# First stage of a two-layer denoising step: modulation by scale columns on TensorE, shift columns on VectorE, and another order of loads

## The chip, the cores and the metric

One core of a Trainium2 chip runs the whole kernel. The metric is device time in microseconds (us), the median of a few executions; lower is better. The core has five engines that each work through their own list in program order: TensorE (PE in the rows; PEld is its weight load), VectorE (DVE), ScalarE (ACT), GpSimd (POOL) and SyncE (SP), which issues the loads.

## The reference

Two groups of tokens (128 context tokens and 256 latent tokens, 384 together) pass through two layers. The part that the change touches is the first of three sub-layers of layer 0:

```
mod  = silu(cond) @ w_mod[l] + b_mod[l]          # cond: one vector of 1024 for each of the 2 groups
h    = x * (1 + mod[scale]) + mod[shift]         # scale and shift: 1024 values each
x    = LN(alpha*x + 0.5*mod[gate] * swiglu(h, w_ffn_in, w_ffn_out))
```

All of it is float32. The kernel makes the large products out of three products of a rounded type: weights and activations are split into a high part and a remainder (`wh` and `wl`, `xh` and `xl`), and `wh*xh + wl*xh + wh*xl` is summed.

## The kernel before

Activations lie with the 1024 features on 8 tiles of 128 partitions (k = 0 to 7) and the 384 tokens along the row. Weights arrive as units of 128 x 1024 in tiles named `raw`, a ring of 8. For a unit u, ScalarE casts `raw` to `wh` (L345) and VectorE subtracts to get `wl` (L353); TensorE then runs 24 products of 128x384, three for each k (L407, L408, L409). `take(n)` prepares units up to n. `dma_w(n)` issues unit loads up to n. All loads of this stage are issued by SyncE in program order; a load that reuses a ring slot waits for the last reader of that slot, and the loads behind it wait too.

The first stage, `first_group`, has to make scale and shift before it can multiply. It goes in four blocks b = 0 to 3 of 256 features (two tiles k each). For a block, `mod_mm` multiplies the conditioning vector `scz` with four loaded pieces of `w_mod` (L980, float32, 8 products of 512 columns for scale and shift together); ScalarE copies the result out of PSUM (`mr`, L987), `mod_sel` turns rows into columns on TensorE (L991), VectorE adds the bias (`ab`, L994 and L995), and `split_mod` makes `xh` on ScalarE (L843) and `hf` and then `xl = hf - xh` on VectorE (L850, L854). `main(u0, u1, k0, k1)` runs the products of units u0 to u1-1 for tiles k0 to k1-1. Seven units belong to the stage: 7 x 24 = 168 products. The order is written out by hand at the end of `first_group`, the products of ready tiles standing between the steps of the modulation.

Later modulation columns come from VectorE: a `w_mod` tile is multiplied with `scb`, the silu of the conditioning vector spread over all partitions, and summed along the row (`mod_dve`, two instructions of L454, one for each group, with a short read of the accumulator). `scb` is loaded by two broadcast loads in `start_rest` and passed through silu on ScalarE (L957).

Of the kernel before, what the change touches and what calls it, by code (L numbers as in the profile page):

```python
# [173 lines left out]
def _pack_mod(a, jobs):  # L174
    out = np.zeros((len(jobs), 128, 1024), np.float32)
    for n, (s, j, mode) in enumerate(jobs):
        l, i = divmod(s, 3)
        c0 = 3 * i * D + 128 * j
        w = a["w_mod"][l]
        if mode == "dve":  # L180
            out[n] = w[:, c0:c0 + 128].T
        else:
            b = j - 4096
            out[n] = np.stack([_blk(w, 2 * mode, 2, i0 + 256 * b, 256).reshape(128, 2, 256) for i0 in (0, D)],
                              axis=2).reshape(128, 1024)
    return out
# [35 lines left out]
C_ID, C_COS, C_SIN, C_INV, C_SEL = 0, 128, 384, 640, 640 + 784  # L222
# [17 lines left out]
class Kernel:  # L240
# [684 lines left out]
    def start(self):  # L925
        nc, io = self.nc, self.io
        self.P = self.t([128, NPAR], name="P")
        self.C = self.t([128, NCONST], name="C")
        self.X = self.t([128, 8, NT], name="X")
        self.scb = self.t([128, 2, 1024], name="scb")  # L930
        self.junk = self.t([128, 1024], BF16, name="junk")
        self.scz = self.t([128, 8, 32], name="scz")
        self.scT = self.scz[:, :, 0:2]
        self.sel = self.C[:, C_SEL:C_SEL + 2]
        self.ones = self.t([128, 1], name="ones")
        self.ident = self.C[:, C_ID:C_ID + 128]
        nc.vector.memset(self.scz, 0.0)
        nc.vector.memset(self.ones, 1.0)
        nc.sync.dma_start(self.P[:, 0:16], io["params"][:, 0:16])
        self.first = [[self.mod_dma(0, 4096, q) for q in range(3)]]  # L940
        nc.sync.dma_start(self.C[:, C_SEL:NCONST], io["const"][:, C_SEL:NCONST])
        nc.sync.dma_start(self.P[:, 16:PC["lng", 0, 0]], io["params"][:, 16:PC["lng", 0, 0]])
        self.first[0].append(self.mod_dma(0, 4096, 3))
        nc.sync.dma_start(self.X[:, 0:2, :], io["x"][:, 0:2, :])
        nc.scalar.activation(self.scT, self.P[:, 0:16].rearrange("p (k c) -> p k c", c=2), AF.Silu)

    def start_rest(self):

        nc, io = self.nc, self.io
        for c in range(2):  # L950
            nc.sync.dma_start(self.scb[:, c, :], io["cond"][c:c + 1, :].to_broadcast([128, D]))
            self.dma_w(self.n_dma + 1)
        nc.sync.dma_start(self.P[:, PC["lng", 0, 0]:NPAR], io["params"][:, PC["lng", 0, 0]:NPAR])
        nc.sync.dma_start(self.C[:, 0:C_SEL], io["const"][:, 0:C_SEL])

        def silu(c):
            nc.scalar.activation(self.scb[:, c, :], self.scb[:, c, :], AF.Silu)  # L957
        self.at(1, lambda: silu(0))
        self.at(1, lambda: silu(1))

    def first_group(self, l, j):

        nc = self.nc
        ab = self.pool.tile([128, 2, 8, 2], F32, name=self.nm("ab"), tag="ab", bufs=2)
        bm = self.par(("bmod", 0), 32).rearrange("p (j c) -> p j c", c=2)
        keys = [("ffn_in", l, j, c) for c in (0, NF, 1, NF + 1, 2, NF + 2, 3)]
        outs = [self.bank() for _ in range(6)] + [self.sbank("mm")]
        mm = nc.tensor.matmul
        ws, xs, psb = [], [], {}

        def load(b):
            self.first.append([self.mod_dma(0, 4096 + b, q) for q in range(4)])
            nc.sync.dma_start(self.X[:, 2 * b:2 * b + 2, :], self.io["x"][:, 2 * b:2 * b + 2, :])

        def mod_mm(b, half):
            if half == 0:
                psb[b] = self.sbank("m0")
            for k in range(4 * half, 4 * half + 4):
                g = 32 * (k % 4)
                mm(psb[b][g:g + 32, :], self.scz[:, k, :],  # L980
                   self.first[b][k // 2][:, 512 * (k % 2):512 * (k % 2) + 512], start=k < 4, stop=k >= 4)

        def mod_sel(b):
            ps = psb[b]
            row = [self.slot(name="mr") for _ in range(2)]
            for h in range(2):
                nc.scalar.copy(row[h][:, 0:256], ps[:, 256 * h:256 * h + 256])  # L987
            sv = self.sbank("m1")
            for h in range(2):
                for c in range(2):  # L990
                    mm(sv[:, 4 * h + 2 * c:4 * h + 2 * c + 2], row[h][:, 128 * c:128 * c + 128], self.sel,  # L991
                       start=True, stop=True)
            s2 = slice(2 * b, 2 * b + 2)
            nc.vector.tensor_add(ab[:, 1, s2, :], sv[:, 0:4].rearrange("p (k c) -> p k c", c=2), bm[:, 2 * b:2 * b + 2])  # L994
            nc.vector.scalar_tensor_tensor(ab[:, 0, s2, :], sv[:, 4:8].rearrange("p (k c) -> p k c", c=2), 1.0,  # L995
                                           bm[:, 8 + 2 * b:10 + 2 * b], ALU.add, ALU.add)
            fin = [self.split_mod(self.X[:, k, :], ab, k) for k in (2 * b, 2 * b + 1)]
            xs.extend(f() for f in fin)

        def main(u0, u1, k0, k1):  # L1000
            for u in range(u0, u1):
                (wh, wl), o = ws[u], outs[u]
                for k in range(k0, k1):
                    sl = slice(128 * k, 128 * k + 128)
                    self.mm3(o[:, :NT], wh[:, sl], wl[:, sl], xs[k][0], xs[k][1], k == 0, k == 7)

        def take(n):
            ws.extend(self.group(keys[len(ws):n]))
            self.held = min(n, self.NW)

        self.dma_w(2)
        load(1)
        self.dma_w(5)
        mod_mm(0, 0)
        mod_mm(0, 1)
        mod_sel(0)
        take(2)
        load(2)
        self.dma_w(7)
        main(0, 1, 0, 2)  # L1020
        mod_mm(1, 0)
        mod_mm(1, 1)
        main(1, 2, 0, 1)
        mod_sel(1)
        main(1, 2, 1, 2)
# [12 lines left out]
        self.dma_w(8)
        self.start_rest()
        main(0, 2, 4, 6)  # L1040
        mod_mm(3, 0)
        mod_mm(3, 1)
        main(2, 4, 4, 6)
        mod_sel(3)
        main(4, 7, 4, 6)
# [668 lines left out]
```

## Time and profile before

| | us |
|---|---|
| median of 3 runs | 1728.32 (1727.93 to 1728.36) |
| the profiled execution | 1728.01 |
| its span | 1726.2 |
| what lies around the span | 1.8 |
| TensorE busy | 1692.5 (98%) |
| the 168 products of the first stage | from 15.8 to 59.1 |

The profiled execution agrees with the runs within 0.3 us, so durations of the trace may be added to the median. TensorE is the engine of the chain that ended last for 90% of the span. A busy share near 100% does not say that TensorE does needed work all the time: the products of the modulation count as busy too.

### The profile page before, as it was taken

What the parts mean: (1) busy time and instruction counts of PE and PEld (TensorE: products, weight loads), DVE (VectorE), ACT (ScalarE), POOL (GpSimd) and SP (SyncE); (2) the same over time, 40 slices, a digit from 0 to 9 for tenths busy, and PEclk for the clock granted to TensorE, in tenths of its full rate; (3) what the DMA queues carried; (4) which work ended last, traced back from release to release, by engine and by line L of the source; (5) the groups of instructions that cost most, each with busy time, mean ns of one, the idle gap of its engine ahead of it and who ended that gap; (6) DMA issues with size and microseconds to landing.
All of it is one profiled execution on the core that took longest, in us unless ns stands there. A gap on an engine that the chain in (4) does not pass through costs nothing.

```text
span 1726.2 us, 26047 instructions
## 1 busy us (share of the span) xinstructions
PE 1692.5 (98%) x9734; PEld 1665.3 (96%) x9734; DVE 1321.2 (77%) x2241; ACT 769.5 (45%) x1369; POOL 342.9 (20%) x410
## 2 busy tenths in 40 slices
PE   7999999999998999999999999999999999999997
PEld 4999999999998999999999999999999999999997
DVE  3699998799959688889777888968998677653433
ACT  3523333656553473333374333347466337433322
POOL 0000023243214510002320000425221363000022
PEclk9999999999999999999999999999999999999998
DMA  9677776435534247676636766753444333544320
GB/s 375 241 236 231 235 233 210 131 110 162 146 114 135 62 140 238 209 213 207 200 99 211 214 206 208 221 160 107 145 138 131 111 116 92 171 148 124 119 75 37
DMA packets 86638, 287.44 MB, mean 167 GB/s; under 512 B 10096, under 2 KB 17520, under 8 KB 86512
## 3 DMA queue, kind: packets, MB, share of 16 engines
q1 hardware_dynamic: 86512, 285.79, 53.2%
q8 instruction: 76, 1.25, 0.3%
q14 instruction: 50, 0.41, 0.1%
HBM read 280.51 MB, written 2.62 MB: 164 GB/s over the span
## 4 chain that ended last, share of the span: by engine, by line
PE 90%; DVE 6%; ACT 2%; issue 1%; DMA 0%; SPq 0%; POOL 0%; ACTq 0%; DVEq 0%; POOLq 0%
PE mm L407 26%; PE mm L408 26%; PE mm L409 26%; DVE wl L353 3%; PE mm L731 1%; PE mm L732 1%; PE mm L734 1%; PE mm L429 1%; PE mm L432 1%; PE mm L430 1%; DVE acc L1117 1%; ACT wh L345 1%; PE m L980 1%; PE sm L539 1%; PE tot L546 1%
## 5 line engine op out<-in xcount | busy, mean ns | idle before, releaser
L345 ACT CAST wh<-raw 128x1024 fp32r<-128x1024 f32 (+3 forms) x430 | 400.3, 948 | 689.8 <-issue 444.2
L407 PE MATMUL mm<-xh,wh 128*128 128x384 f32 x1796 | 608.7, 339 | 4.1 <-ACT wh L345 3.1
L408 PE MATMUL mm<-xh,wl 128*128 128x384 f32 x1796 | 607.1, 338 | 0.6 <-DVE wl L353 0.6
L409 PE MATMUL mm<-xl,wh 128*128 128x384 f32 x1796 | 606.3, 338 | 0.1
L353 DVE TENSOR_TENSOR wl<-raw,wh 128x1024 fp32r<-128x1024 f32 (+3 forms) x430 | 489.8, 1154 | 112.4 <-ACT wh L345 112.2
L407 PEld LDWEIGHTS mm<-xh,wh 128*128 128x128 f32 x1796 | 337.8, 188 | 8.3 <-ACT wh L345 4.1
L408 PEld LDWEIGHTS mm<-xh,wl 128*128 128x128 f32 x1796 | 337.9, 188 | 1.9 <-DVE wl L353 1.8
L409 PEld LDWEIGHTS mm<-xl,wh 128*128 128x128 f32 x1796 | 337.6, 188 | 0.7 <-DVE xl L854 0.7
L454 DVE SCALAR_TENSOR_TENSOR junk<-raw,scb 128x1024 bf16<-128x1024 f32 x256 | 312.7, 1222 | 4.5
L409 PE MATMUL mm<-al,wh 128*128 128x384 f32 x704 | 237.5, 337 | 0.0
L407 PE MATMUL mm<-ah,wh 128*128 128x384 f32 x704 | 237.5, 337 | 0.0
L408 PE MATMUL mm<-ah,wl 128*128 128x384 f32 x704 | 237.3, 337 | 0.0
L625 POOL TENSOR_SCALAR sq<-sq 128x384 f32<-128x384 f32 x6 | 8.5, 1423 | 775.0 <-ACT sq L622 767.3
L409 PEld LDWEIGHTS mm<-al,wh 128*128 128x128 f32 x704 | 132.3, 188 | 0.0
L408 PEld LDWEIGHTS mm<-ah,wl 128*128 128x128 f32 x704 | 132.3, 188 | 0.0
L407 PEld LDWEIGHTS mm<-ah,wh 128*128 128x128 f32 x704 | 132.2, 188 | 0.0
L875 DVE TENSOR_TENSOR al<-a,ah 128x384 fp32r<-128x384 f32 x88 | 48.6, 557 | 80.2 <-ACT ah L874 76.6
L870 DVE TENSOR_TENSOR a<-mm,si 128x384 f32<-128x384 f32 x82 | 45.5, 556 | 75.9 <-ACT si L868 71.0
L1117 DVE SCALAR_TENSOR_TENSOR acc<-U,P,acc 128x399 f32<-128x399 f32 x120 | 87.5, 781 | 0.0
L631 POOL TENSOR_TENSOR s<-s,X 128x384 f32<-128x384 f32 x30 | 39.6, 1320 | 148.9 <-DVE X L611 126.2
L854 POOL TENSOR_TENSOR xl<-hf,xh 128x384 fp32r<-128x384 f32 x40 | 44.6, 1130 | 102.9 <-DVE t L792 84.8
L661 DVE SCALAR_TENSOR_TENSOR yl<-X,ab,yh 128x128 fp32r<-128x128 f32 x80 | 58.7, 770 | 6.2 <-ACT yh L659 6.0
(284 smaller groups left out, 2067.9 us busy)
## 6 DMA issues: line engine op xcount, KB each, us to landing
raw<-in_units SPq DMA_DIRECT2D x356, 512.0 KB, 3.9
raw<-in_wmod SPq DMA_DIRECT2D x144, 512.0 KB, 4.5
raw<-in_units SPq DMA_DIRECT2D x32, 384.0 KB, 3.8
X<-in_x SPq DMA_DIRECT2D x4, 384.0 KB, 7.0
K<-K SPq DMA_DIRECT2D x16, 96.0 KB, 4.3
out_y<-X SPq DMA_DIRECT2D x8, 192.0 KB, 1.8
scb<-in_cond SPq DMA_DIRECT2D x2, 512.0 KB, 7.3
Q<-QL SPq DMA_DIRECT2D x16, 64.0 KB, 3.9
```

The source lines that it names most:

```text
L345: self.nc.scalar.copy(w[0][:, c], r[:, c])
L353: self.nc.vector.tensor_sub(wl[:, c], r[:, c], wh[:, c].bitcast(F32))
L407: mm(out, wh, xh, start=first, stop=False)
L408: mm(out, wl, xh, start=False, stop=False)
L409: mm(out, wh, xl, start=False, stop=last)
L454: self.nc.vector.scalar_tensor_tensor(self.junk, r, 1.0, self.scb[:, c, :], ALU.mult, ALU.mult, accum_out=mv[:, j, c:c + 1])
L631: nc.gpsimd.tensor_add(st["s1"], st["s1"], x)
L661: nc.vector.scalar_tensor_tensor(lo[:, a:b], x[:, a:b], self.ab[:, 0, m, c:c + 1], h[:, a:b].bitcast(F32), ALU.mult, ALU.subtract)
L854: (nc.gpsimd if pool else nc.vector).tensor_sub(xl, hf, xh.bitcast(F32))
L870: nc.vector.tensor_mul(a, u[:, :NT], sl)
L875: nc.vector.tensor_sub(lo, a, h.bitcast(F32))
L1117: nc.vector.scalar_tensor_tensor(acc[c][:, :399], U[c][:, j:j + 399], w, acc[c][:, :399], ALU.mult, ALU.add)
```

## The change

Block 0 is as before (512 columns, scale and shift by TensorE), but for blocks 1 to 3 TensorE multiplies for the scale alone (`scale_mm`, 8 products of 256 columns, two loaded pieces in place of four), and the six shift tiles j = 2 to 7 are each a `w_mod` tile loaded in the transposed form (`col`) and summed by VectorE (`dot`, that is `mod_dve`). For that, `scb` is needed early: `spread` makes it by 16 products of 128 columns on TensorE, a column of `scz` repeated 128 times against the identity, and VectorE copies the result from PSUM. The two broadcast loads of 512 KB and the two silu passes go away; the identity (64 KB) is loaded early. `xl` is made by GpSimd in place of VectorE. `main` runs all `wh` products of a unit ahead of its `wl` products. The third unit's cast and subtraction are taken ahead of the second block.

```diff
-        self.first = [[self.mod_dma(0, 4096, q) for q in range(3)]]
+        self.first = [self.mod_dma(0, 4096, 0)]
+        nc.sync.dma_start(self.C[:, 0:128], io["const"][:, 0:128])
+        self.first += [self.mod_dma(0, 4096, q) for q in (1, 2, 3)]
...
-        for c in range(2):
-            nc.sync.dma_start(self.scb[:, c, :], io["cond"][c:c + 1, :].to_broadcast([128, D]))
...
+        def spread(c, half):
+            b = self.bank()
+            for n in range(4):
+                k = 4 * half + n
+                mm(b[:, 128 * n:128 * n + 128], self.scz[:, k, c:c + 1].to_broadcast([128, 128]), self.ident,
+                   start=True, stop=True)
+            nc.vector.tensor_copy(self.scb[:, c, 512 * half:512 * half + 512], b)
...
+        def scale_mm(b):
+            ps = self.sbank("m0")
+            for k in range(8):
+                g = 32 * (k % 4)
+                mm(ps[g:g + 32, 0:256], self.scz[:, k, :], chunks[b][k // 4][:, 256 * (k % 4):256 * (k % 4) + 256],
+                   start=k < 4, stop=k >= 4)
+            return ps
...
+        def split(k):
+            xs.append(self.split_mod(self.X[:, k, :], ab, k, False, True)())
...
+                for n, (i, w) in enumerate(((0, wh), (1, wh), (0, wl))):
+                    for k in range(k0, k1):
+                        mm(o[:, :NT], w[:, 128 * k:128 * k + 128], xs[k][i], start=n == 0 and k == 0,
+                           stop=n == 2 and k == 7)
...
+        take(3)
+        self.dma_w(4)
+        dot(3)
+        col(5)
+        main(2, 3, 0, 2)
+        self.dma_w(5)
+        sv = columns(scale_mm(1), 1)
+        coef(1, mv[:, 2:4, :], kc(sv[:, 0:4]))
+        split(2)
+        split(3)
+        scale_dma(2)
+        x_dma(2)
+        main(0, 3, 2, 4)
...
+        main(4, 5, 0, 4)
+        sv = columns(scale_mm(2), 1)
+        coef(2, mv[:, 4:6, :], kc(sv[:, 0:4]))
+        split(4)
+        split(5)
+        scale_dma(3)
+        x_dma(3)
+        main(0, 2, 4, 6)
...
+        main(5, 6, 0, 6)
+        sv = columns(scale_mm(3), 1)
+        coef(3, mv[:, 6:8, :], kc(sv[:, 0:4]))
+        split(6)
+        split(7)
+        take(7)
+        main(6, 7, 0, 6)
...
         main(0, 7, 6, 8)
```

TensorE's list, before, around the column step of block 3 (`m_417`); `xh_330` and `xh_337` are tiles k = 4 and 5, made from block 2:

```order
L407 MATMUL mm_89<-xh_337,wh_220 128x384
L408 MATMUL mm_89<-xh_337,wl_221 128x384
L409 MATMUL mm_89<-xl_338,wh_220 128x384
L991 MATMUL m_417<-C_64,mr_413 128x2 x2
L991 MATMUL m_417<-C_64,mr_414 128x2 x2
L407 MATMUL mm_90<-xh_330,wh_266 128x384
L408 MATMUL mm_90<-xh_330,wl_267 128x384
L409 MATMUL mm_90<-xl_331,wh_266 128x384
```

Behind the column step stand products of tiles that are ready already. The same list of the change around block 2, where `xh_325` and `xh_333` are tiles k = 4 and 5, made from the column step `m_320` itself:

```order
L1023 MATMUL mm_154<-xh_236,wl_288 128x384
L993 MATMUL m_309<-raw_244,scz_68 32x256 x4
L993 MATMUL m_309<-raw_246,scz_68 32x256 x4
L1004 MATMUL m_320<-C_64,mr_318 128x2 x2
L1023 MATMUL mm_150<-xh_325,wh_157 128x384
L1023 MATMUL mm_150<-xh_333,wh_157 128x384
L1023 MATMUL mm_150<-xl_326,wh_157 128x384
L1023 MATMUL mm_150<-xl_334,wh_157 128x384
L1023 MATMUL mm_150<-xh_325,wl_158 128x384
```

Here the column step follows the scale products at once, and the next product reads what comes out of it.

VectorE's list, before, from the first subtraction of a unit to the second block's bias step (`ab_85<-m_191`):

```order
L353 TENSOR_TENSOR wl_149<-raw_93,wh_148 128x1024
L353 TENSOR_TENSOR wl_152<-raw_95,wh_151 128x1024
L994 TENSOR_TENSOR ab_85<-m_191,P_63 128x4
L995 SCALAR_TENSOR_TENSOR ab_85<-m_191,P_63 128x4
L850 TENSOR_SCALAR hf_200<-X_65,ab_85 128x128
```

The same stretch of the change; `scb_66` is the spread conditioning vector, `raw_113` and `raw_117` the first two transposed tiles, `mm_138` and `mm_144` the spread products of the second group:

```order
L973 COPY scb_66<-mm_138 128x512
L973 COPY scb_66<-mm_144 128x512
L355 TENSOR_TENSOR wl_158<-raw_109,wh_157 128x1024
L852 TENSOR_SCALAR hf_163<-X_65,ab_86 128x128
L852 TENSOR_SCALAR hf_163<-X_65,ab_86 128x256
L355 TENSOR_TENSOR wl_181<-raw_111,wh_180 128x1024
L456 SCALAR_TENSOR_TENSOR junk_67,mv_87<-raw_113,scb_66 128x1024 x2
L355 TENSOR_TENSOR wl_195<-raw_115,wh_194 128x1024
L456 SCALAR_TENSOR_TENSOR junk_67,mv_87<-raw_117,scb_66 128x1024 x2
L1010 TENSOR_TENSOR ab_86<-mv_87,P_63 128x4
```

Two copies, one more unit and four summing instructions have moved ahead of the second bias step.

## Rows read from the trace of the kernel before

**Rows 1.** The page: span and instructions of the profiled execution.

```profile
span 1726.2 us, 26047 instructions
```

**Rows 2.** Busy us (x instructions) of PE, PEld, DVE, ACT, POOL, then PEclk, DMA, GB/s.

```profile
59.10:300.00 240.90, 240.90 (x1383) 240.90 (x1383) 220.59 (x348) 85.08 (x130) 25.12 (x25) 1.00 0.72 225
```

**Rows 3.** Groups from 15.8 to 59.1 us: count | busy us, mean ns | idle before.

```profile
L407 PE MATMUL mm<-xh,wh 128*128 128x384 f32 x57 | 20.6, 361 | 3.9 <-ACT wh L345 3.1 <-ACT xh L843 0.7
...
L980 PE MATMUL m<-raw,scz 128*32 128x512 f32 x48 | 6.8, 671 | 0.0
```

**Rows 4.** Timeline of block 0, all engines: start, duration, instruction, [idle before].

```profile
5.09 6.04 PE L980 MATMUL m<-raw,scz 128*32 128x512 f32 x16 [5.09 <-DMA raw<-in_wmod]
...
9.81 0.19 PEld L980 LDWEIGHTS m<-raw,scz 128*32 128x32 f32 x4 [1.54 <-DMA raw<-in_wmod]
...
11.60 1.05 PE L991 MATMUL m<-C,mr 128*128 128x2 f32 x8 [0.47 <-ACT mr L987]
...
12.96 1.86 ACT L843 ACTIVATE xh<-X,ab 128x128 fp32r<-128x128 f32 x4 [1.13 <-DVE ab L995]
12.96 1.25 DVE L850 TENSOR_SCALAR hf<-X,ab 128x128 f32<-128x128 f32 x4
...
14.73 1.98 ACT L345 CAST wh<-raw 128x1024 fp32r<-128x1024 f32 x2
...
15.79 2.36 DVE L353 TENSOR_TENSOR wl<-raw,wh 128x1024 fp32r<-128x1024 f32 x2 [0.38 <-ACT wh L345]
15.81 0.29 PEld L407 LDWEIGHTS mm<-xh,wh 128*128 128x128 f32 x1 [3.24 <-ACT wh L345]
```

**Rows 5.** Timeline of block 1 behind its column step.

```profile
23.58 1.86 ACT L843 ACTIVATE xh<-X,ab 128x128 fp32r<-128x128 f32 x4 [1.13 <-DVE ab L995]
...
24.61 0.44 PE L407 MATMUL mm<-xh,wh 128*128 128x384 f32 x1 [0.71 <-ACT xh L843]
```

**Rows 6.** Timeline of block 3, TensorE.

```profile
43.63 1.92 PE L980 MATMUL m<-raw,scz 128*32 128x512 f32 x16
...
47.70 0.95 PE L991 MATMUL m<-C,mr 128*128 128x2 f32 x8
48.51 0.42 PE L407 MATMUL mm<-xh,wh 128*128 128x384 f32 x1
```

**Rows 7.** GpSimd's subtraction: shortest/median/longest of 40 (ns, first and last start).

```profile
L854 POOL TENSOR_TENSOR xl<-hf,xh x40: 1010/1022/1846, 321.5 to 1454.2; 128x384 fp32r<-128x384 f32 x40
```

**Rows 8.** Timeline of VectorE and GpSimd where such a subtraction is long.

```profile
330.50 1.21 DVE L353 TENSOR_TENSOR wl<-raw,wh 128x1024 fp32r<-128x1024 f32 x1
...
330.75 1.84 POOL L854 TENSOR_TENSOR xl<-hf,xh 128x384 fp32r<-128x384 f32 x1 [0.57 <-DVE hf L850]
```

**Rows 9.** Timeline of VectorE's two summing instructions of one tile.

```profile
69.06 1.22 DVE L454 SCALAR_TENSOR_TENSOR junk<-raw,scb 128x1024 bf16<-128x1024 f32 x1
...
70.32 1.23 DVE L454 SCALAR_TENSOR_TENSOR junk<-raw,scb 128x1024 bf16<-128x1024 f32 x1
```

**Rows 10.** Timeline of TensorE: three products against the identity (two records each).

```profile
89.21 0.83 PE L539 MATMUL sm<-C,y 128*128 128x128 f32 x6
89.80 0.42 PE L407 MATMUL mm<-xh,wh 128*128 128x384 f32 x1
```

**Rows 11.** The page's group of VectorE reading PSUM, 384 columns.

```profile
L870 DVE TENSOR_TENSOR a<-mm,si 128x384 f32<-128x384 f32 x82 | 45.5, 556 | 75.9 <-ACT si L868 71.0
```

**Rows 12.** Stretches as in rows 2, for the granted clock (third figure from the end).

```profile
14.00:16.00 2.00, 0.19 (x1) 0.19 (x1) 1.45 (x4) 2.00 (x4) 0.00 (x0) 0.50 1.03 412
...
590.70:594.10 3.40, 3.40 (x13) 3.40 (x13) 2.72 (x18) 0.63 (x2) 0.00 (x0) 0.50 0.52 149
...
1431.00:1433.00 2.00, 2.00 (x16) 2.00 (x17) 1.86 (x6) 1.47 (x5) 0.00 (x0) 1.00 0.00 0
```

**Rows 13.** Timeline of TensorE: first of four alike groups of statistics products, two places.

```profile
588.34 0.72 PE L546 MATMUL tot<-ones,s 128*128 128x1 f32 x6
...
1429.48 0.72 PE L546 MATMUL tot<-ones,s 128*128 128x1 f32 x6
```

More of the change, by code (lines that the diff above doesn't have):

```diff
@@ L181, in _pack_mod @@
             out[n] = w[:, c0:c0 + 128].T
+        elif mode in ("sc0", "sc1"):
+            out[n] = _blk(w, 4 * int(mode[2]), 4, D + 256 * (j - 4096), 256)
         else:
@@ L939, in start @@
         nc.sync.dma_start(self.P[:, 0:16], io["params"][:, 0:16])
-        self.first = [[self.mod_dma(0, 4096, q) for q in range(3)]]
+        self.first = [self.mod_dma(0, 4096, 0)]
+        nc.sync.dma_start(self.C[:, 0:128], io["const"][:, 0:128])
+        self.first += [self.mod_dma(0, 4096, q) for q in (1, 2, 3)]
         nc.sync.dma_start(self.C[:, C_SEL:NCONST], io["const"][:, C_SEL:NCONST])
         nc.sync.dma_start(self.P[:, 16:PC["lng", 0, 0]], io["params"][:, 16:PC["lng", 0, 0]])
-        self.first[0].append(self.mod_dma(0, 4096, 3))
         nc.sync.dma_start(self.X[:, 0:2, :], io["x"][:, 0:2, :])
@@ L949, in start_rest @@
         nc, io = self.nc, self.io
-        for c in range(2):
-            nc.sync.dma_start(self.scb[:, c, :], io["cond"][c:c + 1, :].to_broadcast([128, D]))
-            self.dma_w(self.n_dma + 1)
         nc.sync.dma_start(self.P[:, PC["lng", 0, 0]:NPAR], io["params"][:, PC["lng", 0, 0]:NPAR])
[L954 to L959, printed above, removed]
+        nc.sync.dma_start(self.C[:, 128:C_SEL], io["const"][:, 128:C_SEL])
     def first_group(self, l, j):
@@ L966, in first_group, with col, dot, scale_dma @@
         keys = [("ffn_in", l, j, c) for c in (0, NF, 1, NF + 1, 2, NF + 2, 3)]
-        outs = [self.bank() for _ in range(6)] + [self.sbank("mm")]
         mm = nc.tensor.matmul
-        ws, xs, psb = [], [], {}
-        def load(b):
-            self.first.append([self.mod_dma(0, 4096 + b, q) for q in range(4)])
+        ws, xs, raws, chunks = [], [], {}, {}
+        mv = self.mvt(0)
+        def spread(c, half):
[5 more added lines that the diff above has]
+            nc.vector.tensor_copy(self.scb[:, c, 512 * half:512 * half + 512], b)
+        def col(*js):
+            for jj in js:
+                raws[jj] = self.mod_dma(0, jj, "dve")
+        def dot(*js):
+            for jj in js:
+                self.mod_dve(0, jj, raws.pop(jj))
+        def scale_dma(b):
+            chunks[b] = [self.mod_dma(0, 4096 + b, m) for m in ("sc0", "sc1")]
+        def x_dma(b):
             nc.sync.dma_start(self.X[:, 2 * b:2 * b + 2, :], self.io["x"][:, 2 * b:2 * b + 2, :])
[L975 to L978, printed above, removed]
+        def scale_mm(b):
+            ps = self.sbank("m0")
+            for k in range(8):
                 g = 32 * (k % 4)
[L980 to L986, printed above, removed]
+                mm(ps[g:g + 32, 0:256], self.scz[:, k, :], chunks[b][k // 4][:, 256 * (k % 4):256 * (k % 4) + 256],
+                   start=k < 4, stop=k >= 4)
+            return ps
+        def columns(ps, n):
+            row = [self.slot(name="mr") for _ in range(n)]
+            for h in range(n):
                 nc.scalar.copy(row[h][:, 0:256], ps[:, 256 * h:256 * h + 256])
             sv = self.sbank("m1")
-            for h in range(2):
+            for h in range(n):
                 for c in range(2):
@@ L992, in mod_sel, with coef @@
                        start=True, stop=True)
+            return sv
+        def coef(b, shift, scale):
             s2 = slice(2 * b, 2 * b + 2)
[L994 to L998, printed above, removed]
+            nc.vector.tensor_add(ab[:, 1, s2, :], shift, bm[:, 2 * b:2 * b + 2])
+            nc.vector.scalar_tensor_tensor(ab[:, 0, s2, :], scale, 1.0, bm[:, 8 + 2 * b:10 + 2 * b], ALU.add, ALU.add)
+        def split(k):
+            xs.append(self.split_mod(self.X[:, k, :], ab, k, False, True)())
+        kc = lambda v: v.rearrange("p (k c) -> p k c", c=2)
         def main(u0, u1, k0, k1):
@@ L1002, in main @@
                 (wh, wl), o = ws[u], outs[u]
-                for k in range(k0, k1):
-                    sl = slice(128 * k, 128 * k + 128)
-                    self.mm3(o[:, :NT], wh[:, sl], wl[:, sl], xs[k][0], xs[k][1], k == 0, k == 7)
+                for n, (i, w) in enumerate(((0, wh), (1, wh), (0, wl))):
+                    for k in range(k0, k1):
+                        mm(o[:, :NT], w[:, 128 * k:128 * k + 128], xs[k][i], start=n == 0 and k == 0,
+                           stop=n == 2 and k == 7)
         def take(n):
@@ L1009, in take @@
             self.held = min(n, self.NW)
-        self.dma_w(2)
-        load(1)
-        self.dma_w(5)
[L1014 to L1025, printed above, removed]
+        ps = self.sbank("m0")
+        for q in range(4):
+            for k in (2 * q, 2 * q + 1):
+                g = 32 * (k % 4)
+                mm(ps[g:g + 32, :], self.scz[:, k, :], self.first[q][:, 512 * (k % 2):512 * (k % 2) + 512],
+                   start=k < 4, stop=k >= 4)
+            if q in (1, 2):
+                spread(0, q - 1)
@@ new lines, in first_group @@
+        self.dma_w(2)
+        col(2)
+        self.dma_w(3)
+        col(3)
+        sv = columns(ps, 2)
+        coef(0, kc(sv[:, 0:4]), kc(sv[:, 4:8]))
+        split(0)
+        for h in range(2):
+            spread(1, h)
+        outs = [self.bank() for _ in range(6)] + [self.sbank("mm")]
+        take(1)
+        split(1)
+        scale_dma(1)
+        x_dma(1)
+        main(0, 1, 0, 2)
+        take(2)
+        dot(2)
+        col(4)
+        main(1, 2, 0, 2)
+        take(3)
+        self.dma_w(4)
@@ L1026, in first_group @@
+        dot(3)
+        col(5)
+        main(2, 3, 0, 2)
+        self.dma_w(5)
+        sv = columns(scale_mm(1), 1)
[5 more added lines that the diff above has]
+        main(0, 3, 2, 4)
         take(4)
-        main(0, 2, 2, 4)
-        main(2, 3, 0, 4)
-        mod_mm(2, 0)
+        dot(4)
+        col(6)
         main(3, 4, 0, 4)
         take(5)
-        load(3)
-        mod_mm(2, 1)
+        self.dma_w(6)
+        dot(5)
@@ L1034, in first_group @@
+        col(7)
         main(4, 5, 0, 4)
+        sv = columns(scale_mm(2), 1)
[5 more added lines that the diff above has]
+        main(0, 2, 4, 6)
+        take(6)
+        dot(6)
+        self.dma_w(7)
+        main(2, 5, 4, 6)
+        dot(7)
+        main(5, 6, 0, 6)
[3 more added lines that the diff above has]
+        split(7)
         take(7)
-        mod_sel(2)
@@ L1037, in first_group @@
-        main(5, 7, 0, 4)
+        main(6, 7, 0, 6)
         self.dma_w(8)
         self.start_rest()
[L1040 to L1045, printed above, removed]
         self.held = 5
```

## Prediction

> **What bounds the kernel now.** I read the page first, for the span [rows 1], then the busy times by stretch, then the timeline of the first stage. From 59.1 us on TensorE is busy in all 240.9 us that the row covers, 1383 instructions at 0.174 us each [rows 2]; it waits for nobody there, and the change leaves the instructions behind the first stage as they were. So what the change is worth is decided by one date: when TensorE has run the 168 products of the first stage. Before, that is 59.1 us: 57, 56 and 56 products of the three kinds have started by then [rows 3], and the 169th is the first of the next unit. The first product starts at 15.8 [rows 4], and 168 x 0.174 = 29.2 us, so 14.1 us of that stretch go to modulation and waiting: the modulation products of blocks 1 to 3 are busy for about 6.8 us [rows 3], the rest is column steps and idle time. DMA is not what bounds the end: it has the last modulation piece there before TensorE comes to it at 43.6 [rows 6], and the amount loaded by then is nearly the same in both kernels (the two 512 KB loads that go away came later).
>
> What the reader should see is how a block's chain is covered before. In block 3 the column step ends and the next product starts at 48.51, 0.8 us after the column step's start, because it needs none of it [rows 6]. In block 1 it is not covered: ScalarE starts `xh` at 23.58 and TensorE's next product comes at 24.61, 1.03 us later, with the wait put down to `xh` [rows 5].
>
> **The change part by part.** I work out dates from block 0's rows and go on in program order.
>
> *Start.* The fourth modulation piece ends TensorE's first run at 5.09 + 6.04 = 11.13 [rows 4]. The identity's 64 KB go ahead of it now, but 144 KB of parameters go behind it; I keep 11.13. The first two spreads (4 products each, 0.79 us each by 0.59 us for three products [rows 10]) fit into waits for pieces, of which the last is 1.54 us [rows 4]: nothing. Without that cover they would cost 1.6 us. The column step ends at 12.65, `xh` starts at 12.96. The other two spreads run to 14.25, when nothing else is ready: nothing on TensorE.
>
> *VectorE up to the second bias step.* This is its queue: `hf` 12.96 to 13.58 (half of 1.25 [rows 4]); two PSUM copies, bounded below by 0.56 and taken as 0.56 x 512/384 = 0.74 [rows 11], to 15.06; `wl` of unit 0, half of 2.36 [rows 4], to 16.24; `hf` to 16.86; `wl` of unit 1 to 18.04. GpSimd's `xl` wants to start at 16.9. Alone it takes 1.02, beside such a `wl` up to 1.84 [rows 7, 8], so it ends at 18.75, and I let the next summing instruction wait for that. Two of these take 2.5 (1.26 from start to start [rows 9]): 21.25; `wl` of unit 2: 22.43; two more: 24.93; bias step 0.31 (12.65 to 12.96 [rows 4]): 25.24. The GPSIMD Engine Reference of the Trainium skill, section Key points, says that GpSimd contends with VectorE instructions of two SBUF inputs; rows 8 agree for `wl`, and no row here shows it for the summing instruction, which also has two. If that one did not wait, VectorE would be ready 0.7 us earlier and TensorE's chain, next, would decide.
>
> *TensorE up to there.* The 18 products of units 0 to 2 on tiles 0 and 1 wait for `wl` of unit 2 (22.43) and end at 22.78. The scale products are half of block 3's 1.92 [rows 6], 0.96 (from 0.48, if halving the columns saves more, to 1.92, if it saves nothing): 23.74. Copy 0.47 (11.13 to 11.60) and half a column step, 0.52 [rows 4]: 24.73. VectorE's 24.93 comes last, by 0.2.
>
> *Each block's chain is now bare.* Behind the bias step, with `xh` starting at T: first `xh` and first product at T + 1.03 [rows 5], second `xh` 0.93 later [rows 4], but the first `xl` follows the first `xh` by 1.02 and the second `xl` by another 1.02 [rows 7]: the fourth product starts at T + 3.0. Block 1: 28.25. Then 15 of 18 products, and 24 of units 3 and 4 (their `wl` at 29.4 and 33.1 come in time): 39 x 0.174 to 35.04. Block 2: scale products to 36.00, copy 36.47, column step 36.99, T = 37.30, fourth product 40.30. VectorE has finished its sums at 35.6, 1.4 us ahead of the bias step. Then 45 products: 48.13. Block 3: 49.09, 49.56, 50.08, T = 50.39; unit 6 needs none of its tiles, but its cast stands behind both `xh` on ScalarE: 1.86, and 384 of 1024 columns of a cast of 0.99 [rows 4], 0.37, so 52.7. Then 60 products: 63.1. That is **4.0 us later** than 59.1. The three bare chains hold 3.5, 3.3 and 3.1 us in which TensorE runs nothing, 9.8 in all.
>
> *Clock.* In such gaps the clock can fall from 2.4 to 1.2 GHz. It stood at 0.50 at 14 to 16 us after block 0's idle time, and from 590.7 to 594.1 after four groups of one-column products from 588.34 on; but after the same four groups from 1429.48 on it stayed at 1.00 [rows 12, 13]. The new gaps are longer than those stretches, 3.7 to 4.5 us from the scale products to dense work, so I take two falls of three. One lasts 3.4 us at half rate [rows 12], which costs 1.7 us where products stand dense and 1.5 with a little of it in the gap: 3.0 us.
>
> *Other parts.* No silu passes on ScalarE, no 1 MB load: off the path, nothing. `wh` products ahead of `wl`: counted above. Ring slots: SyncE's loads now wait for sums too, with the last pieces and `x` tiles queued behind them; the slowest, of the third block's scale pieces, waits for the sum ending at 35.6 and lands some 4 us later, 8 us ahead of its product. If the sums came 8 us later, block 3 would be late.
>
> **Sum.** 4.0 + 3.0 = 7.0 us. Span 1726.2 + 7.0 [rows 1], 1.8 around it: 1735.0. The profiled execution stands 0.3 below the median of the runs, so the forecast is 1735.3.
>
> **Rivals.**
> *No fall of the clock, or one.* For: one of two like stretches left it alone. 1732.3 to 1733.8.
> *All three fall,* each with its full 1.7: 4.0 + 5.1 = 9.1, 1737.4, and up to 2.9 more if scale products cost 1.92. For: the gaps are longer than the stretch at 588. By TensorE: Matmul & The Clock Gate of the Trainium skill, section HAM oscillation, a matmul burst that ends in a long wait leaves the clock low at each following burst, which is this case; the trace has one fall and one stay for it.
> *Faster.* TensorE finds other work during the chains, as block 3 before [rows 6]: without the 9.8 us the stage ends at 53.3, 5.8 early: 1722.5. It decides from 4.0 of the 9.8 on. Against: TensorE's rows behind blocks 1 and 2 read the new tiles at once, and rows 5 show it waiting in that place. The page just named, section Part 2, says that matmuls stay in program order and only weight loads are pulled ahead; no row contradicts it.
> *No gain and no loss.* Half of the gaps disappear because `xl` and casts come earlier than I sum, or because scale products cost 0.48: 1728 to 1731.8.
>
> **How the numbers follow.** I give two falls 0.45, none or one 0.25, three 0.15, no difference 0.09, faster 0.06. Within 0.2% (3.5 us, about what a measurement of this kernel tells from no change) lies the fourth case alone: slower 0.85, same 0.09, faster 0.06. Leaving out faster, most of no difference and the top of three falls, the range is 1731.6 to 1739.5; it takes in the bounds of the scale products (-1.4 to +2.9) beside two falls.
>
> **What would show it.** Right: TensorE idle three times in the first stage, each between a column step and the first product, with the wait put down to `xh`, `xl` of GpSimd or the cast; the first product of unit 7 near 66 us; granted clock at 0.5 in two stretches between 24 and 57 us; no new waits later. Wrong: dense products right behind the column steps; TensorE waiting for modulation pieces; the second bias step far from 25 us, which would put VectorE's queue or GpSimd at fault; or a wait behind 66 us that I did not see.

## The result, and the profile after

The changed kernel takes 1743.29 us (median of 4 runs, 1740.24 to 1745.45) against 1728.34 for the kernel before on the same chip: ratio 1.0081, 95% interval 1.0070 to 1.0093. It is slower, as forecast, but by 15 us (14.0 by the ratio) where 7 were worked out, and outside the range. The profiled execution took 1742.66 us; the line of the page that answers to [rows 1]:

```profile
span 1741.0 us, 26124 instructions
```

The first stage, 59.1 us before, now ends at 75.2. In the table by stretch, with the columns of [rows 2], the first row is the stage, the second the 240.9 us behind it, the last four are stretches with the clock at half:

```profile
18.40:75.20 56.80, 44.66 (x229) 39.53 (x230) 35.92 (x66) 19.71 (x39) 9.13 (x8) 0.82 0.76 255
75.20:316.10 240.90, 240.90 (x1381) 240.90 (x1380) 220.41 (x348) 85.06 (x130) 24.82 (x25) 1.00 0.72 225
21.80:28.60 6.80, 4.93 (x15) 4.66 (x15) 6.54 (x10) 0.00 (x0) 1.81 (x1) 0.50 0.73 236
32.10:38.80 6.70, 6.24 (x17) 5.37 (x18) 5.09 (x8) 2.77 (x5) 2.02 (x2) 0.50 0.86 292
49.10:52.50 3.40, 3.40 (x12) 3.40 (x12) 3.33 (x8) 0.00 (x0) 0.00 (x0) 0.50 0.99 397
62.80:66.10 3.30, 2.87 (x9) 2.87 (x10) 2.89 (x6) 3.30 (x9) 1.18 (x2) 0.50 0.20 79
```

Behind the stage TensorE is busy without a gap, as it was in [rows 2]: no new wait stands there, and the loss is made in the first 75 us. Within them the clock is at half (0.50 of 2.4 GHz is its level of 1.2) in four stretches, 20.5 us together by the clock's records. The groups of TensorE in the stage, which answer to [rows 3]:

```profile
L1023 PE MATMUL mm<-xh,wh 128*128 128x384 f32 x56 | 18.0, 420 | 6.6 <-ACT xh L845 3.6 <-ACT wh L347 2.9
L1023 PE MATMUL mm<-xl,wh 128*128 128x384 f32 x56 | 17.1, 400 | 4.5 <-POOL xl L856 4.5
...
L993 PE MATMUL m<-raw,scz 128*32 128x256 f32 x48 | 3.2, 385 | 0.0
L1004 PE MATMUL m<-C,mr 128*128 128x2 f32 x12 | 1.8, 256 | 1.5 <-ACT mr L1000 1.5
```

TensorE waits 6.6 + 4.5 + 1.5 = 12.6 us, for `xh`, the cast, GpSimd's `xl` and the copy `mr` ahead of the column steps; [rows 3] has 3.9 for the first kind of product, 3.1 of them ahead of the stage's first product. The timeline of TensorE from its first product to the column step of block 0, which answers to [rows 4]:

```profile
4.98 1.92 PE L1035 MATMUL m<-raw,scz 128*32 128x512 f32 x4 [4.98 <-DMA raw<-in_wmod]
7.65 1.92 PE L1035 MATMUL m<-raw,scz 128*32 128x512 f32 x4 [0.75 <-DMA raw<-in_wmod]
9.50 2.08 PE L971 MATMUL mm<-C,scz 128*128 128x128 f32 x8
11.51 1.05 PE L1035 MATMUL m<-raw,scz 128*32 128x512 f32 x4
12.49 1.16 PE L971 MATMUL mm<-C,scz 128*128 128x128 f32 x8
13.58 1.05 PE L1035 MATMUL m<-raw,scz 128*32 128x512 f32 x4
15.10 0.27 PE L1004 MATMUL m<-C,mr 128*128 128x2 f32 x1 [0.47 <-ACT mr L1000]
```

From 7.65 on it waits for no piece: the spreads (L971) stand on the path with 2.08 + 1.16 us, and the column step starts at 15.10 in place of 11.60. Then GpSimd's second `xl`, in the timeline of all engines:

```profile
20.40 1.22 DVE L355 TENSOR_TENSOR wl<-raw,wh 128x1024 fp32r<-128x1024 f32 x1
20.63 2.98 POOL L856 TENSOR_TENSOR xl<-hf,xh 128x384 fp32r<-128x384 f32 x1 [2.12 <-DVE hf L852]
...
21.54 1.22 DVE L456 SCALAR_TENSOR_TENSOR junk<-raw,scb 128x1024 bf16<-128x1024 f32 x1
...
22.80 1.89 DVE L456 SCALAR_TENSOR_TENSOR junk<-raw,scb 128x1024 bf16<-128x1024 f32 x1
23.66 0.29 PEld L1023 LDWEIGHTS mm<-xl,wh 128*128 128x128 f32 x1 [4.05 <-POOL xl L856]
23.66 0.69 PE L1023 MATMUL mm<-xl,wh 128*128 128x384 f32 x1 [3.73 <-POOL xl L856]
```

The subtraction lies beside a `wl` and a whole summing instruction and takes 2.98 us; TensorE waits 3.73 us for it, and the clock falls in that wait. Block 3, all engines:

```profile
60.08 0.61 PE L1004 MATMUL m<-C,mr 128*128 128x2 f32 x4 [0.49 <-ACT mr L1000]
60.72 0.16 DVE L1011 SCALAR_TENSOR_TENSOR ab<-m,P 128x4 f32<-128x4 f32 x1 [5.53 <-PE m L1004]
60.92 1.86 ACT L845 ACTIVATE xh<-X,ab 128x128 fp32r<-128x128 f32 x4 [0.90 <-DVE ab L1011]
...
63.23 2.29 PE L1023 MATMUL mm<-xh,wh 128*128 128x384 f32 x6 [2.55 <-ACT wh L347]
```

This is the bare chain: column step, bias step, `xh`, cast, and TensorE idle for 2.55 us, where in [rows 6] it had a product to run 0.8 us behind the column step's start. VectorE stood at its bias step for 5.53 us, so its sums were long done.

### The profile page after: what moved, and what is told of

Its sections match the earlier page's. It is cut to its first block, busy times and chain, and to the rows that moved or that the text cites. A ratio compares the mean times of both kernels' runs of the same rounds, so it can differ in the third digit from the quotient of the medians.

```text
span 1741.0 us, 26124 instructions
## 1 busy us (share of the span) xinstructions
PE 1698.4 (98%) x9754; PEld 1673.9 (96%) x9754; DVE 1337.2 (77%) x2261; ACT 767.0 (44%) x1364; POOL 353.3 (20%) x418
## 4 chain that ended last, share of the span: by engine, by line
PE 87%; DVE 6%; ACT 2%; issue 1%; DMA 0%; POOL 0%; ACTq 0%; SPq 0%; DVEq 0%; POOLq 0%
PE mm L409 25%; PE mm L410 25%; PE mm L411 25%; DVE wl L355 2%; PE mm L733 1%; PE mm L734 1%; PE mm L736 1%; PE mm L431 1%; PE mm L434 1%; PE mm L432 1%; DVE acc L1172 1%; ACT wh L347 1%; PE mm L1023 1%; PE sm L541 1%; PE tot L548 1%
## 5 line engine op out<-in xcount | busy, mean ns | idle before, releaser
L409 PE MATMUL mm<-xh,wh 128*128 128x384 f32 x1740 | 588.7, 338 | 0.4 <-ACT e L1534 0.2
L410 PE MATMUL mm<-xh,wl 128*128 128x384 f32 x1740 | 587.0, 337 | 0.0
L411 PE MATMUL mm<-xl,wh 128*128 128x384 f32 x1740 | 585.9, 337 | 0.0
L456 DVE SCALAR_TENSOR_TENSOR junk<-raw,scb 128x1024 bf16<-128x1024 f32 x268 | 328.0, 1224 | 4.7
L409 PEld LDWEIGHTS mm<-xh,wh 128*128 128x128 f32 x1740 | 326.6, 188 | 0.8 <-ACT e L1534 0.7
L410 PEld LDWEIGHTS mm<-xh,wl 128*128 128x128 f32 x1740 | 326.8, 188 | 0.6 <-DVE wl L355 0.6
L411 PEld LDWEIGHTS mm<-xl,wh 128*128 128x128 f32 x1740 | 326.8, 188 | 0.0
L856 POOL TENSOR_TENSOR xl<-hf,xh 128x384 fp32r<-128x384 f32 x48 | 54.7, 1154 | 154.9 <-DVE t L794 83.2
```

The costliest lines, as they stand in the source:

```text
L409: mm(out, wh, xh, start=first, stop=False)
L410: mm(out, wl, xh, start=False, stop=False)
L411: mm(out, wh, xl, start=False, stop=last)
L456: self.nc.vector.scalar_tensor_tensor(self.junk, r, 1.0, self.scb[:, c, :], ALU.mult, ALU.mult, accum_out=mv[:, j, c:c + 1])
L856: (nc.gpsimd if pool else nc.vector).tensor_sub(xl, hf, xh.bitcast(F32))
```

## The experiments

Theory A: TensorE's uncovered chains, and the falls of the clock that they cause, make the loss, the spreads' place the rest. Rivals: B, VectorE's sums are late; C, GpSimd's subtraction; D, the start alone. Ratios are to runs of the kernel before on the same chip (medians 1728.3 to 1730.4), and what is said below to be won or lost "by the ratios" is their difference times 1729 us. Times in us; the stage is done when its 168 products have started; stretches at half clock within it, from the clock's first rise on, are given by start and length. The last three columns are of one execution, the profiled one: against its kernel's median this lies 3.3 us lower in cover23, 2.1 lower in cover_all and 2.5 higher in hybrid, elsewhere within 2 us. Between the stage and the last 30 us the profiles have none to two more stretches at half clock, near 600, 1400 or 1440 us (none in the change, two in cover23), so totals also differ by what the table does not show.

| kernel | median | ratio, 95% interval | column step of block 0 | stage done | clock at half |
|---|---|---|---|---|---|
| before | 1728.34 | 1 | 11.60 | 59.1 | 13.8 (6.8) |
| the change | 1743.29 | 1.0081, 1.0070 to 1.0093 | 15.10 | 75.2 | 21.8 (6.8), 32.0 (6.8), 49.1 (3.4), 62.8 (3.4) |
| xl_vector | 1742.61 | 1.0077, 1.0065 to 1.0089 | 15.83 | 75.4 | 27.0 (10.2), 47.5 (3.4), 61.2 (6.8) |
| late_spread | 1741.02 | 1.0069, 1.0057 to 1.0081 | 11.34 | 72.2 | 18.9 (6.8), 32.5, 46.2, 59.8 (3.4 each) |
| cover23 | 1738.27 | 1.0048, 1.0036 to 1.0060 | 13.61 | 63.8 | 19.2 (6.8), 32.8 (3.4) |
| fill_gaps | 1740.03 | 1.0060, 1.0048 to 1.0072 | 15.65 | 71.0 | 22.5 (6.8) |
| no_sums | 1745.20 | 1.0090, 1.0077 to 1.0103 | 17.40 | 76.9 | 25.3 (3.4), 32.2 (6.8), 49.2 (3.4), 62.9 (6.8) |
| cover_all | 1732.29 | 1.0016, 1.0007 to 1.0025 | 11.66 | 61.1 | 19.1 (3.4), 29.3 (3.4) |
| before_xl_pool | 1733.96 | 1.0017, 1.0009 to 1.0026 | 11.60 | 61.5 | 16.2 (6.8), 26.4 (3.4) |
| spread_only | 1744.36 | 1.0079, 1.0066 to 1.0093 | 12.85 | 77.4 | 24.0 (6.8), 37.7, 51.3, 65.0 (3.4 each) |
| cover_fill | 1731.63 | 1.0003, 0.9995 to 1.0012 | 11.29 | 60.2 | 26.5 (3.4) |
| hybrid | 1732.11 | 1.0014, 1.0004 to 1.0024 | 11.97 | 60.3 | 24.5 (3.4), 38.1 (3.4) |
| hybrid2 | 1725.73 | 0.9981, 0.9970 to 0.9992 | 11.40 | 55.5 | 24.1 (3.4) |
| hybrid2_fill | 1725.75 | 0.9978, 0.9969 to 0.9987 | 11.58 | 56.4 | none |

**xl_vector.**

```diff
-            xs.append(self.split_mod(self.X[:, k, :], ab, k, False, True)())
+            xs.append(self.split_mod(self.X[:, k, :], ab, k)())
```

> The change with one edit: VectorE instead of GpSimd makes xl in the first stage. After the change TensorE waits 3.7 us for GpSimd's second xl at 19.9 to 23.7 us, and the granted clock falls at 21.8 while it waits. Theory (bare chains, and the clock that falls in them): that wait shrinks to below 1 us, and if the fall at 21.8 goes with it another 2 us come back; in blocks 1 to 3 the xl of VectorE is shorter than the one of GpSimd, so the fourth product comes about 0.5 us sooner in each. 1738 to 1741 against the change's 1743.3. If GpSimd's subtraction is the main cause of the loss: 1733 or below. If VectorE's queue is the bound, eight more subtractions there make it slower: 1744 to 1748.

The interval of the ratio lies almost on that of the change: nothing won that can be told, and the median is above the 1741 that A allowed. The waits of TensorE in block 0 and ahead of the scale products of block 1:

```profile
22.39 0.44 PE L1023 MATMUL mm<-xl,wh 128*128 128x384 f32 x1 [1.74 <-DVE xl L856]
...
27.07 1.01 PE L1023 MATMUL mm<-xh,wl 128*128 128x384 f32 x2 [2.15 <-DVE wl L355]
```

The 3.73 us for GpSimd have become 1.74 + 2.15 for VectorE, whose queue is longer by the subtractions, and the clock falls all the same. C is out as the main cause; so is A's expectation of some 2 us from this edit.

**late_spread.**

```diff
-            if q in (1, 2):
-                spread(0, q - 1)
...
-        for h in range(2):
-            spread(1, h)
+        for c in range(2):
+            for h in range(2):
+                spread(c, h)
```

and in the loads the identity behind the fourth piece.

> The change with one edit: the loads of the first block in the order of before, the identity's 64 KB behind the fourth modulation piece, and all four spreads behind the column step of block 0. If the column step of block 0 is late because of the two spreads and the identity's load (15.1 against 11.6 us), it starts near 11.6 again. What the later spreads push back on VectorE (two copies of 0.7 us) lies ahead of the first subtraction. Theory: 2 to 3.5 us faster than the change, 1740 to 1741.5, because the start is one part of the loss only. If the start were the main cause, also through the clock: 1735 or below. If the column step stays at 15 us, something else holds it.

The column step is back at 11.34 and the stage ends 3.0 us sooner; the total is 2.1 us lower by the ratios, with intervals that overlap. D holds for its size only. Of the 3.8 us won at the start some went to GpSimd's second `xl` again: all four copies now stand in VectorE's queue ahead of `wl` and the second `hf`, and the wait is longer than the 3.73 of the change:

```profile
21.68 0.69 PE L1023 MATMUL mm<-xl,wh 128*128 128x384 f32 x1 [5.09 <-POOL xl L856]
```

**spread_only**, half of that edit: spreads late, identity still ahead of the second piece.

> The change with all four spreads behind the column step of block 0, but the identity's load still ahead of the second modulation piece: half of the edit that brought the column step from 15.1 back to 11.34 us. If the first two spreads hold TensorE (2.1 and 1.2 us at half rate), the column step starts at 11.3 to 12.5. If the identity's load delays the pieces, it starts at 13 or later. The total, 1740 to 1742, should not tell much, since wherever the column step falls VectorE's and GpSimd's first subtractions come behind it.

The column step starts at 12.85, between the two, and between the two cases that I had set. In the five kernels with both it starts 0.8 to 4.5 us later still (13.61 to 17.40). How much of the 1.5 us over late_spread's 11.34 is the identity's place can't be told: TensorE waited 0.88 us for the second piece, but the clock's first rise also came at 20.6 us here, in late_spread at 8.6 and in the change at 11.5, so that all four pieces ran at half rate. The total, 2.4 us above what I allowed, gave nothing back; that the late rise is the reason is not shown.

**cover23.**

```diff
-        main(4, 5, 0, 4)
-        sv = columns(scale_mm(2), 1)
+        ps = scale_mm(2)
+        main(3, 4, 0, 4)
+        sv = columns(ps, 1)
...
+        main(4, 5, 0, 4)
         main(0, 2, 4, 6)
```

and in the same way `scale_mm(3)` ahead of `main(2, 5, 4, 6)`, with the column step and `take(7)` ahead of `main(5, 6, 0, 6)`.

> The change with the order written otherwise: the scale products of blocks 2 and 3 stand ahead of a group of products of ready tiles (24 products of 4.2 us in block 2 at full clock, 18 or more in block 3), and the column steps with what follows stand behind that group; casts and sums are moved ahead as this needs. Nothing is added or left out. Theory (the bare chains of blocks 2 and 3 cost their idle time and let the clock fall): TensorE's idle time there falls from about 6 us to under 3, two of the four stretches at half clock get shorter or vanish: 1732 to 1737 against 1743.3. If VectorE's queue of sums is the bound, the same wait stands a few instructions later: above 1741. If the loss were all at the start and in block 1: 1742 to 1744.

5.7 us faster than the change by the ratios (0.0033 x 1729), the stage done 11.3 us sooner in the profiled execution, the fastest of five, of which 1.5 are its earlier start; the median lies 1.3 above the upper end that I gave. The stretches of blocks 1 to 3:

```profile
28.30:43.10 14.80, 12.57 (x69) 10.71 (x69) 10.46 (x22) 6.69 (x13) 3.50 (x4) 0.88 0.87 294
43.10:49.70 6.60, 6.08 (x44) 5.19 (x44) 6.50 (x10) 2.03 (x6) 0.53 (x1) 1.00 1.03 392
49.70:63.80 14.10, 14.10 (x83) 14.10 (x83) 8.88 (x21) 7.92 (x16) 2.05 (x2) 1.00 0.82 296
```

From block 3's column step at 49.70 TensorE has no gap left and the clock stays at 1.00. Nothing but order was changed, so the bare chains of blocks 2 and 3, with their falls of the clock, are shown to be a large part of the loss: 5.7 of 14.0 us by the ratios, 9.8 of 16.1 at the stage's end of the two profiles. B is out there.

**fill_gaps**, and its core:

```diff
+        def fill(sv, n):
+            for _ in range(n):
+                mm(sv[:, 128:512], ws[0][0][:, 0:128], xs[0][0], start=True, stop=True)
```

> The change with 28 products of 128x384 added that nobody reads (7, 7 and 14 behind the column steps of blocks 1, 2 and 3, into unused columns of the column step's bank): they stand where TensorE waits for xh and xl. They add 28 x 0.174 = 4.9 us of work at full clock, and no wait is taken away. Theory, with the clock as the larger part of the loss in blocks 1 to 3: the falls at 32, 49 and 63 us (in which products stand 0.32 apart) vanish or get shorter, and this gives back more than the filling costs: 1737 to 1741. If the clock does not fall because of the waits, or costs little: 1743 to 1748, the filling lying partly in the waits.

The kernel with 28 products more is 3.6 us faster (0.0021 x 1729; the two intervals just touch), as A has it. The stretches from column step to column step, and the fall at 22.5 that has no filling:

```profile
30.90:43.40 12.50, 11.00 (x69) 9.37 (x70) 8.79 (x16) 4.12 (x7) 2.01 (x2) 1.00 0.89 279
43.40:57.00 13.60, 12.13 (x75) 10.50 (x75) 8.42 (x17) 3.36 (x8) 2.02 (x2) 1.00 0.92 328
57.00:71.00 14.00, 13.71 (x79) 13.62 (x80) 8.79 (x18) 9.10 (x19) 2.04 (x2) 1.00 0.67 226
22.50:29.30 6.80, 5.09 (x15) 4.66 (x15) 6.38 (x10) 0.00 (x0) 1.65 (x1) 0.50 0.72 233
```

In the change the same three stretches take 14.6, 15.2 and 15.1 us: 4.8 us more, with the same chains and 28 products fewer. So in blocks 1 to 3 the waits make the clock fall. The section HAM oscillation of the Trainium skill's page TensorE: Matmul & The Clock Gate describes this kind of loss, bursts that each end in a wait and begin again cold; the change agrees with it in blocks 1 to 3, though its waits there, at most 2.55 us, are shorter than the DMA waits of the page's example. In the five kernels with all three chains bare (the change, xl_vector, late_spread, no_sums, spread_only) every one of the fifteen lies in a stretch at half clock or is followed by one within 5 us of its column step; no chain of blocks 2 and 3 that is covered or filled has such a fall (hybrid's, below, waits for a bare cast).

**no_sums.**

```diff
-                self.mod_dve(0, jj, raws.pop(jj))
+                nc.vector.tensor_copy(mv[:, jj, :], raws.pop(jj)[:, 0:2])
```

> The change with VectorE's twelve summing instructions of the shift tiles left out (six copies of two columns stand for them, so the shift of blocks 1 to 3 is not computed). VectorE's queue is shorter by about 12 x 1.25 = 15 us over the stage. Rival (VectorE's sums set the date of the bias steps): 1733 to 1737 against the change's 1743.3. Theory (the chains themselves are bare, VectorE waits for TensorE's column step 2.5 to 5.5 us in blocks 1 to 3): only block 1 gains, where the sums lie beside GpSimd's second xl, 1739 to 1742.

No gain, and a miss of A's own number too. The column step of block 0 started at 17.40 here (a wait of 1.97 us for the second piece), 2.3 us later than in the change's profile. From there to block 1's it took 13.4 us in place of 15.2, the gain expected. The later blocks gain nothing: TensorE has the waits of the change there to 0.01 us (1.27, 0.44 and 0.53 in block 2, 2.55 in block 3), and VectorE waits for TensorE's column step, 8.64 and 10.31 us. In block 1 it is:

```profile
30.77 0.61 PE L1004 MATMUL m<-C,mr 128*128 128x2 f32 x4 [0.49 <-ACT mr L1000]
31.42 0.16 DVE L1011 SCALAR_TENSOR_TENSOR ab<-m,P 128x4 f32<-128x4 f32 x1 [5.20 <-PE m L1004]
```

B is out: without any sums it is 59.5 us from block 0's column step to the end of the stage, with them 60.1.

**before_xl_pool**, the kernel before with `xl` by GpSimd (`split_mod(..., False, True)`).

> The kernel before with one edit: GpSimd instead of VectorE makes xl in the first stage. If GpSimd's subtraction by itself were the loss: 1735 or above. Theory: VectorE is relieved of eight subtractions, GpSimd is passed over by the two-input instructions of VectorE in blocks 0 and 1 and the first xl product comes up to 2 us later there; within 1727 to 1731.

2.9 us slower than the kernel before, a miss for A, which gave 1731 at most: the stage ends 2.4 us later, with a second fall of the clock at 26.4. GpSimd's subtraction is thus a loss by itself; in the change it only stood in one wait with others, as xl_vector shows.

**cover_all**, the edits of cover23, late_spread and xl_vector together.

> The change with the three edits together: covered column steps of blocks 2 and 3, spreads behind the column step of block 0 with the loads in the order of before, xl by VectorE. Theory: the parts add up, and the first stage ends within 3 us of the 59.1 of before or ahead of it: 1723 to 1732. If the loss had another cause that none of the three touches (loads, the summing of the shift), it stays at 1735 or above.

All but 2.8 us of the loss is gone, and the median lies 0.3 above the upper end that I gave. What is left lies in blocks 0 and 1: both stretches at half clock, and TensorE's waits of 2.63 us for the second `xl` and 1.27 for `xh`, come ahead of block 2's column step at 37.30; behind it the longest wait is 0.35 us.

**cover_fill**, the same with `fill` in two places, 14 and 7 products.

> The kernel with the three edits together (covered column steps of blocks 2 and 3, late spreads, xl by VectorE), and 21 products of 128x384 that nobody reads: 14 where TensorE waits 2.6 us for the second xl of block 0, 7 behind the column step of block 1. In the kernel without them the granted clock is at half from 19.1 and from 29.3 us, 3.4 us each. If the clock falls because of these waits: both stretches vanish, the first stage ends some 2 to 3 us sooner, near 58.5, and the total is 1728 to 1730.5 against 1732.4. If it falls for another reason, the stage ends at 61 or later.

One fall remains, behind a wait of 2.15 us for `wl`, and the stage ends at 60.2, not 58.5. The ratio can't be told from the kernel before, nor for sure from cover_all. Which of the two waits made which fall isn't told apart by it.

**hybrid**, in its core (spreads behind the column step of block 0, `take(2)`, then the copies; blocks 2 and 3 with `scale_mm` and sums):

```diff
+        chunks[1] = [self.mod_dma(0, 4097, q) for q in range(4)]
...
+        main(0, 1, 0, 2)
+        ps = both_mm(chunks[1])
+        main(1, 2, 0, 1)
+        sv = columns(ps, 2)
+        coef(1, kc(sv[:, 0:4]), kc(sv[:, 4:8]))
+        split(2, 3)
+        main(1, 2, 1, 2)
```

> Another division: blocks 0 and 1 and the order of products as before, the shift by VectorE only for blocks 2 and 3 (four tiles, eight sums in place of twelve), xl by VectorE, the four spreads in TensorE's wait of 3.2 us behind the column step of block 0, their copies behind the second unit's subtraction. The two loads of 512 KB, the silu passes and half of the products of blocks 2 and 3 (about 0.85 us each, 1.92 against 1.07) go away as in the change. Theory: with every column step covered the change's parts cost nothing, and 1.7 us remain as a gain, with 2 more if the spreads keep the clock up from 13.8 us on: first stage done at 55.5 to 57.5, 1724.5 to 1727.5. If the sums themselves load VectorE too much: a wait for the bias step in block 2 or 3, and 1730 or above.

A miss, and for a reason of the same kind: my order put the casts of units 5 and 6 behind block 2's `xh` on ScalarE. TensorE's waits in the stage (us in total, times, longest):

```profile
PE mm L1024 <- ACT wh L347: 2.5, 1, 2.5
PE mm L1024 <- ACT xh L845: 1.1, 2, 0.7
```

**hybrid2**

```diff
+        take(7)
         main(4, 5, 0, 4)
         sv = columns(ps, 1)
         coef(2, mv[:, 4:6, :], kc(sv[:, 0:4]))
         split(4, 5)
-        take(7)
```

> The division with TensorE's shift in blocks 0 and 1, and the casts and subtractions of units 5 and 6 taken ahead of block 2's column step, as the kernel before has them, in place of behind its xh. In the run without this TensorE waited 2.55 us at 38.09 for a cast that stood behind both xh on ScalarE, and the granted clock fell at 38.12. Theory (the same bare cast as in block 3 of the change): wait and fall go together, first stage done at 56 to 57.5 in place of 60.3, and the total 2.5 to 4 us below the run without it, at 1725 to 1729. If the loads of units 5 and 6 are late, the bias step of block 2 waits behind their subtractions, and nothing is gained.

The wait for the cast and the fall behind it are gone together, the stage ends at 55.5, and the kernel is faster than the kernel before, by 3.3 us (0.0019 x 1729; 1.4 to 5.2 by the interval). Its stage in one row:

```profile
15.90:55.50 39.60, 38.43 (x236) 33.87 (x235) 33.03 (x65) 18.81 (x38) 0.00 (x0) 0.96 0.99 384
```

Block 1's column step stands at 19.90 in place of 22.25: the spreads fill TensorE's first wait, and the half clock of [rows 12] at 14 to 16 us doesn't come. More comes from the scale products of two blocks, at 1.07 us in place of 1.92 in [rows 6]; the fall at 24.1 takes some of it back. `main` has the change's order of `wh` and `wl` products here as in all the kernels made from the change; that order was not tried by itself, but it does not keep a kernel from being faster than before.

**hybrid2_fill**, with 8 filling products in block 1.

> The same with 8 products of 128x384 that nobody reads where TensorE waits for xh in block 1 (0.7 and 0.43 us at 22 to 24 us; the granted clock fell at 24.46 there). They cost at most 0.5 us beyond the wait. If this wait made the clock fall: the stretch from 24.5 is gone, 1 us or a little more is won over the run without them. If the fall has an older cause or stays: 0 to 0.5 us slower.

The fall at 24.1 is gone, but the stage ends 0.9 us later, at 56.4, and the ratios are the same. With the 8 products, 1.4 us at full clock, TensorE still comes to block 2's scale products sooner than at hybrid2's 29.12, but it then waits for their two pieces:

```profile
29.03 0.64 PE L993 MATMUL m<-raw,scz 128*32 128x256 f32 x8 [0.90 <-DMA raw<-in_wmod]
30.22 0.64 PE L993 MATMUL m<-raw,scz 128*32 128x256 f32 x8 [0.55 <-DMA raw<-in_wmod]
```

What the fall cost is hidden by this wait for loads: taking it away alone won nothing.

## Why the prediction was wrong in size

The sum's time for the end of the stage was 59.1 + 7.0 = 66.1; it came at 75.2. Its steps in order:

**Start: wrong.** "Nothing" for the first two spreads rested on waits for pieces as cover. The 1.54 us of [rows 4] are idle time of the weight load (PEld); the row of TensorE's products shows none from 5.09 to 11.13, so their cover was less than I read. In the change the one wait for a piece, 0.75 us, comes ahead of the spreads and none lies at them, and the fallback that I named, 1.6 us, took its price from products at full clock; the first spread took 2.08 us, the other 1.16. The column step came 3.5 us late. late_spread shows that the two places, of the spreads and of the identity, are the cause together; their shares stay open.

**VectorE and GpSimd up to the second bias step: right in the sum, wrong in its order.** From the column step's start to the end of the sums it was 13.2 us (15.10 to 28.29) against 13.3 worked out (11.60 to 24.93). But the summing instruction did not wait for GpSimd; it passed it, `xl` took 2.98 us instead of 1.84, and TensorE waited for it. That by itself cost nothing: 23.66 + 15 x 0.174 is 11.2 us behind the column step's start, just where I had the 18 products end. What was lost came behind the wait: the products there ran at half clock, 0.32 us apart.

**The bare chains: right.** Chains of 3.5, 3.3 and 3.1 us were forecast. `xh` started at 31.12, 45.75 and 60.92; the fourth product came 3.1 us later in blocks 1 and 2, against 3.0, and block 3's first product 2.31 later, against 2.3. Waits went to `xh`, GpSimd's `xl` and the cast, as named.

**Clock: the failed term.** I took two falls of 3.4 us, 3.0 us of cost. There were four, two of them 6.8 us long. By the rows of the four stretches 15 + 17 + 12 + 9 = 53 products ran in them, 0.32 us apart in place of 0.174: 53 x 0.146 = 7.7 us, 4.7 more than priced. The step that failed is "so I take two falls of three": one like stretch of two had left the clock alone before, and I carried that rate over to gaps that I had worked out to be longer; measured, all three chains ran into a fall, and so did all fifteen of the five kernels with bare chains. The rival with all three falls had the mechanism and still too short a stretch for it; and the fourth, in GpSimd's wait, stood in no case.

**Together.** 7.0 + 3.5 + 4.7 = 15.2 of 16.1 us at the stage's end; 0.9 I can't place. 1.5 us come back later, because the fall at 590.7 of [rows 12] does not occur in the change: its span is 14.8 us longer. No other wait arose, and loads were no bound, as said.

**The rivals.** "Faster" was the right mechanism for another kernel: with chains covered as in [rows 6] 5.7 of the 14.0 us go in cover23, 11.2 in cover_all, and hybrid2, which leaves the shift of block 1 to TensorE, ends at 55.5 where 53.3 were worked out for the change without idle time. In the change itself nothing covers them.

## What to carry to other kernels

When work is moved off TensorE, look first at what stood behind each column step or reduction in its list: a chain of 3 us that nothing covers costs its own length and, if it comes again and again, about half as much once more through the clock (here (17 + 12 + 9) x 0.146 = 5.5 us beside the 9.8 us of the chains). Price a term in the state in which it will run (the first spread, before the clock had risen, took 2.08 us, the second 1.16), and count a fall for each bare chain rather than an average. With nearly all chains covered, a like division was worth 3.3 us.

## What was not expected of the hardware

- Products that nobody reads made a kernel faster: 28 of them, 3.6 us.
- A GpSimd subtraction of 1.02 us (the median of [rows 7]) took 2.98 beside a `wl` and a summing instruction, and the next summing instruction 1.89 in place of 1.22.
- The clock's first rise came anywhere between 8.5 and 20.6 us in these kernels' profiles, with the first product at 4.8 to 5.1, and with it the length of the first products. What sets it was not tried.
- In block 1 a wait of 0.71 us for `xh` left the clock up in the kernel before; in hybrid2 waits of 0.70 and 0.43 us were followed by a fall, at 24.1 us, which products in that place took away. What tells the two apart stays open.
